# Warming matmuls up to the first scaled rows, and the first norm's factors on a queue of their own

## The chip, the cores and the metric

The kernel runs on one core of one Trainium2 chip. The metric is device time in microseconds (us) of one execution. TensorE (PE) multiplies, VectorE (DVE), ScalarE (ACT) and GpSimd (POOL) work on rows, SyncE (SP) issues DMAs. A core's engines have a queue each and meet through semaphores.

## The reference, cut

All arrays are float32: x is 1 x 512 x 1024, `w_in` 1024 x 6656, the feed-forward inner width 2816.

```python
h = rmsnorm(x, norm1_g)                       # y = x * rsqrt(mean(x^2) + eps) * g
z = h @ w_in + b_in
z_glu, z_rx, z_rg, z_ga, z_gb = split(z)
u = z_glu[:, :1024] * sigmoid(z_glu[:, 1024:])
u = silu(layernorm(causal_depthwise_conv(u, conv_dw_w, conv_dw_b)))
y_a = u @ conv_w_out + conv_b_out
hb = rg_lru(causal_depthwise_conv(z_rx, ...), ...)     # gates per head, a scan over time
y_b = (hb * gelu(z_rg)) @ lru_w_out
x = x + (sigmoid(z_ga) * y_a + sigmoid(z_gb) * y_b) @ w_mix_out
h = rmsnorm(x, norm2_g)
x = x + (silu(h @ ffn_w1) * (h @ ffn_w3)) @ ffn_w2
return rmsnorm(x, norm_f_g)
```

## The kernel before

Activations are kept with channels on partitions: a tile is 128 channels by 512 positions. Each factor of a product is split into a high part in TensorE's faster float32 form and a low part (the remainder), and a product is three matmuls per 128 channels (`mm3`): high by high, high by low, low by high. With `lo_last` the products with the weights' low part come last. Weights come in chunks of 128 x 1024 (`emit_chunk`): SP loads `raw_in`, ScalarE casts the high part (line 122), GpSimd or VectorE subtracts the low part (line 118).

The change lies in the head of the kernel, up to the end of the first four products.

- `load_x(t)`: SP loads rows 128t to 128t+127 of x in two halves of 512 columns.
- `norm1_rows(t)`: ScalarE sums squares over both halves (lines 530 and 536), then takes the square root (537); VectorE inverts it (538) and scales the rows in place (570).
- `turn_half("tx", ...)`: for half of the positions (two t's) and each of the eight channel tiles, TensorE turns two 128 x 128 blocks (554); ScalarE writes the high part h1kh times the norm's factor (557) and VectorE the low part h1kl (558). The factor is a column of `par`.
- `par`: all vectors of parameters, one column per 128 channels. They are loaded as rows (`load_rows`) into row tiles `rows`, turned by TensorE and copied out by VectorE (`rows_turned`, lines 498 and 499). The first row tile holds `norm1_g` (8 rows) and `b_in` (52 rows).
- `early_mm(i, hf)`: the first four products z, each on half of the positions.
- The warming matmuls (line 486) multiply a tile of ones by itself ahead of all that; nobody reads what they write.

In the head the order on PE, ACT, DVE and SP is the one written out by hand (`tc.manual_schedule`); further on a scheduler decides it. SP's queue before: x of t = 0 and 1, the rows of `norm1_g`, the rows of `b_in`, the first two weight chunks, x of t = 2 and 3, a third chunk, all other parameter rows, then more chunks. TensorE's: 12 warming matmuls, the turning of `norm1_g` and `b_in`, tx of the first half, z of two chunks, tx of the second half, z of two more, the turning of all other parameters, and the four products' second halves. In ScalarE's, the cast of the first weight chunk stands between the sums of squares and the factors of tx.

Of the kernel before, what the change touches and what calls it, by code (L numbers as in the profile page):

```python
# [13 lines left out]
P = 128  # L14
# [19 lines left out]
RAW = 4  # L34
HL = 5
AHEAD = 4
WARM = 12

FEW, MANY = 32, 112

# [12 lines left out]
ROWS = [  # L53
    ("norm1_g", 8), ("b_in", 52), ("conv_dw_b", 8), ("conv_ln_g", 8), ("conv_ln_b", 8),
    ("conv_b_out", 8), ("lru_conv_b", 10), ("lru_ba", 10), ("lru_bx", 10),
    ("lru_lambda", 10), ("norm2_g", 8), ("lru_conv_w", 40),
    ("conv_dw_w", 248),
]
# [27 lines left out]
def tile_block(ctx, tc, a, out):  # L86
    nc = tc.nc
# [18 lines left out]
    def bank(name):  # L106
        return psum.tile([P, T], F32, tag="mm", name=name)

    def bank2(name):
        return psum2.tile([P, T], F32, tag="cv", name=name)  # L110

    vec, act, pe, pool_e = nc.vector, nc.scalar, nc.tensor, nc.gpsimd
# [56 lines left out]
    def emit_to(n):  # L169
        while emitted[0] < min(len(chunks), n):  # L170
            emit_chunk()
# [271 lines left out]
    n_rows = sum(n for _, n in ROWS)  # L443
    n_first = ROWS[0][1] + ROWS[1][1]
    par = consts.tile([P, n_rows], F32, name="par")
    row_at = lambda c: (0, c) if c < n_first else (1 + (c - n_first) // P, (c - n_first) % P)
    at, col, parts = 0, {}, []
    for name, n in ROWS:
        col[name] = at
        src = a[name]  # L450
        src = src.rearrange("l k (c p) -> (l k c) p", p=P) if len(src.shape) == 3 else src.rearrange("l (c p) -> (l c) p", p=P)
        done = 0
        while done < n:
            m = min(n - done, P - row_at(at + done)[1])
# [2 lines left out]
        at += n  # L457
    rowt = [longt(f"rows{b}") for b in range(row_at(n_rows - 1)[0] + 1)]

    def load_rows(i):  # L460
        lo, m, src = parts[i]
        b, r = row_at(lo)
        nc.sync.dma_start(rowt[b][r : r + m, :P], src)

    x_nat = a["x"].rearrange("b (t p) d -> p (b t) d", p=P)
    xt = [[longt(f"x{t}{h}") for h in range(2)] for t in range(NT)]
# [1 line left out]
    def load_x(t):  # L468
        for h in range(2):
            nc.sync.dma_start(xt[t][h], x_nat[:, t, h * T : (h + 1) * T])  # L470

    eps_t = consts.tile([P, 1], F32, name="eps_t")
    vec.memset(eps_t, EPS)
# [10 lines left out]
    wp = bank2("warm")  # L484
    for _ in range(WARM):
        pe.matmul(wp[:, :P], ones, ones, start=True, stop=True)

    first = [i for i, (lo, _, _) in enumerate(parts) if lo < n_first]
    load_x(0)
    load_x(1)  # L490
    for i in first:
        load_rows(i)

    def rows_turned(c0, c1):
        pt = bank2(f"par_ps{c0}")
        for c in range(c0, c1, P):
            m = min(P, c1 - c)
            pe.transpose(pt[:, c - c0 : c - c0 + m], rowt[row_at(c)[0]][:m, :P], ident[:m, :m])
        vec.tensor_copy(par[:, c0:c1], pt[:, : c1 - c0])
# [5 lines left out]
    def mm3(ps, ws, xs, lo_last=False):  # L505


        n = 3 * len(ws)
        i = 0
        three = [((wh, xh), (wh, xl), (wl, xh)) for (wh, wl), (xh, xl) in zip(ws, xs)]  # L510
        if lo_last:
            three = [q[:2] for q in three] + [q[2:] for q in three]
        for l, r in (q for qs in three for q in qs):
            pe.matmul(ps, l, r, start=i == 0, stop=i == n - 1)  # L514
            i += 1

    def w_tiles(key, kt, ahead=AHEAD):
        h, l = weights(key, ahead)
        return [(h[:, k, :], l[:, k, :]) for k in range(kt)]
# [21 lines left out]
    def rstd_of(halves, junk, between=None):  # L541
        begun = rstd_begin(halves[0], junk[0])
        if between:
            between()
        return rstd_end(begun, halves[1], junk[1])

    def turn_half(name, rows, gname, dest, hf, bk, some=range(ND)):

        cs = slice(hf * 256, hf * 256 + 256)
        for c in some:  # L550
            ps = bk[c % len(bk)](f"{name}{hf}{c}")
            for t in range(2):
                src = rows[2 * hf + t][c // 4][:, (c % 4) * P : (c % 4 + 1) * P]
                pe.transpose(ps[:, t * P : (t + 1) * P], src, ident)
            g = pc(gname, c)
            h, l = (v[:, cs] for v in dest[c])
            act.activation(h, ps[:, :256], AF.Copy, scale=g)
            last = vec.scalar_tensor_tensor(out=l, in0=ps[:, :256], scalar=g, in1=h.bitcast(F32), op0=ALU.mult, op1=ALU.subtract)
        return last.ins

    def parts_of(pair_tiles, cs=slice(0, T)):
        return [(h[:, cs], l[:, cs]) for h, l in pair_tiles]
# [3 lines left out]
    def norm1_rows(t):  # L566
        junk = [shortt(f"n1j{t}{h}") for h in range(2)]
        r = rstd_of(xt[t], junk)
        for h in range(2):
            vec.tensor_scalar(out=xt[t][h], in0=xt[t][h], scalar1=r, scalar2=None, op0=ALU.mult)  # L570
# [6 lines left out]
    def early_mm(i, hf):  # L577
        m = EARLY_IN[i]
        if hf == 0:
            early.append((m, w_tiles(f"in{m}", ND, 0), bank(f"z{m}")))  # L580
        _, ws, ps = early[i]
        mm3(ps[:, HALVES[hf]], ws, parts_of(h1p, HALVES[hf]), lo_last=hf == 0)
# [3 lines left out]
    with tc.manual_schedule(engines={ET.PE, ET.Activation, ET.DVE, ET.SP}):  # L586
        norm1_rows(0)
        norm1_rows(1)
        rows_turned(0, n_first)
        emit_to(1)  # L590
        turn_half("tx", xt, "norm1_g", h1p, 0, [bank, bank, bank, bank2])
        emit_to(2)
        load_x(2)
        load_x(3)
        norm1_rows(2)
        norm1_rows(3)
        emit_to(3)
        for i in range(len(parts)):
            if i not in first:
                load_rows(i)  # L600
        early_mm(0, 0)
        early_mm(1, 0)
        turn_half("tx", xt, "norm1_g", h1p, 1, [bank2, bank, bank])
        emit_to(4)
        early_mm(2, 0)
        early_mm(3, 0)
        rows_turned(n_first, n_rows)
        for i in range(4):
            early_mm(i, 1)
# [447 lines left out]
    first = {}  # L1057
# [189 lines left out]
```

## Time and profile before

| | us |
|---|---|
| median of 3 runs | 807.54 |
| lowest, highest | 807.03, 810.36 |
| the profiled execution | 807.57 |
| its span, first to last instruction | 805.8 |

A row of a timeline gives the start and the length in us, the engine, the line and the operation, out<-in by the program's names, and in brackets how long the engine had sat idle and what ended that. A row of the chain gives start, length, engine, what and line. A row of stretches gives the stretch, its length, the busy time of engines with the count of their records in brackets, then TensorE's granted clock as a share of full speed, the mean busy share of the DMA engines, and GB/s. Where a line is given, PE and PEld (the loads of weights into TensorE) are of that line alone. PEq, SPq and the like are an engine's own sequencer.

### The profile page before, as it was taken

Reading aid. Unit: us, or ns where it says so; the run is one execution under the profiler, and the core shown is the slowest. Engines: PE = TensorE matmul, PEld = TensorE weight load, DVE = VectorE, ACT = ScalarE, POOL = GpSimd, SP = SyncE. Lnnn points to the kernel's source line nnn. Section 1 sums busy time; section 2 is a strip of 40 time slices with the busy share of each in tenths; the row PEclk is TensorE's granted clock in tenths of the full one; section 3 lists DMA queues with packets and bytes.
Section 4 is the critical chain, followed back from the end, with each engine's and each line's share of the span. In section 5 each row is a group of like instructions: output and inputs, shape, how many; then the busy total and the mean of one; then the engine's idle time right before and its main releaser. Section 6 shows DMA issues by size and latency. Waiting matters only on the chain.

```text
span 805.8 us, 12192 instructions
## 1 busy us (share of the span) xinstructions
PE 790.4 (98%) x4374; PEld 690.7 (86%) x4374; DVE 677.6 (84%) x1026; ACT 471.4 (58%) x677; POOL 234.3 (29%) x184
## 2 busy tenths in 40 slices
PE   8999999999999999999999999999999999999996
PEld 7988888788888888888888888999999999888885
DVE  4699899999989988786788879887878887889756
ACT  7546585988668855563326474454555555577443
POOL 3565867786766855130000000000000000000000
PEclk8999999999999999999999999999999999999999
DMA  7945547377564764468847546667555543676652
GB/s 216 231 122 164 172 149 213 118 233 206 168 188 151 221 179 119 127 207 266 279 155 236 157 130 164 153 160 202 153 141 132 132 131 105 209 260 198 197 169 105
DMA packets 184912, 141.34 MB, mean 175 GB/s; under 512 B 14311, under 2 KB 162195, under 8 KB 184851
## 3 DMA queue, kind: packets, MB, share of 16 engines
q1 hardware_dynamic: 183123, 134.27, 54.9%
q0 software_dynamic: 1728, 6.29, 4.1%
q8 instruction: 34, 0.56, 0.3%
q14 instruction: 27, 0.22, 0.1%
HBM read 113.79 MB, written 18.64 MB: 164 GB/s over the span
## 4 chain that ended last, share of the span: by engine, by line
PE 80%; DVE 8%; DMA 6%; ACT 3%; issue 2%; SPq 0%; ACTq 0%; DVEq 0%; POOLq 0%
PE z L514 29%; PE or L926 13%; PE yb L514 7%; PE fa L1052 6%; PE ft L1052 6%; PE ya L514 5%; PE mxr L926 5%; DMA raw_fb<-raw_fb 3%; DVE cv L673 3%; PE fe L1052 3%; PE fb L1052 2%; DMA raw_fb<-in_ffn_w_dram 2%; PE g L800 2%; PE fr L1052 1%; DVE raw_fb L346 1%
## 5 line engine op out<-in xcount | busy, mean ns | idle before, releaser
L673 DVE SCALAR_TENSOR_TENSOR cv<-u,par,cv 128x511 f32<-128x511 f32 (+16 forms) x240 | 162.1, 729 | 2.7 <-ACT cv L670 2.5
L118 POOL TENSOR_TENSOR hl_in<-raw_in,hl_in 128x1024 fp32r<-128x1024 f32 x52 | 126.0, 2428 | 81.4 <-ACT hl_in L122 78.4
L344 POOL DMA_DIRECT2D raw_fb<-raw_fb x12 | 10.5, 873 | 301.3 <-DMA raw_fb<-in_ffn_w_dram 134.6
L118 POOL TENSOR_TENSOR ows<-ows 128x256 f32<-128x256 f32 x66 | 57.4, 872 | 37.3 <-DMA ows<-in_ffn_w_dram 34.3
L122 ACT CAST hl_ft<-raw_fb 128x1024 fp32r<-128x1024 f32 x40 | 41.7, 1049 | 31.3 <-DVE raw_fb L346 16.7
L122 ACT CAST hl_in<-raw_in 128x1024 fp32r<-128x1024 f32 x52 | 54.2, 1043 | 9.5 <-PE z L514 6.6
L118 DVE TENSOR_TENSOR hl_ft<-raw_fb,hl_ft 128x1024 fp32r<-128x1024 f32 x40 | 48.5, 1218 | 9.3 <-ACT hl_ft L122 9.2
L118 DVE TENSOR_TENSOR hl_fb<-raw_fb,hl_fb 128x1024 fp32r<-128x1024 f32 x30 | 36.6, 1221 | 9.0 <-ACT hl_fb L122 8.8
L514 PE MATMUL z<-h10h,hl_in 128*128 128x512 f32 (+1 forms) x112 | 42.3, 379 | 0.0
L514 PE MATMUL z<-h11h,hl_in 128*128 128x512 f32 (+1 forms) x112 | 41.8, 375 | 0.0
L514 PE MATMUL z<-h14h,hl_in 128*128 128x512 f32 (+1 forms) x112 | 41.8, 375 | 0.0
L514 PE MATMUL z<-h13h,hl_in 128*128 128x512 f32 (+1 forms) x112 | 41.8, 375 | 0.0
L514 PE MATMUL z<-h12h,hl_in 128*128 128x512 f32 (+1 forms) x112 | 41.8, 375 | 0.0
L514 PE MATMUL z<-h15h,hl_in 128*128 128x512 f32 (+1 forms) x112 | 41.8, 375 | 0.0
L514 PE MATMUL z<-h16h,hl_in 128*128 128x512 f32 (+1 forms) x112 | 41.7, 374 | 0.0
L514 PE MATMUL z<-h17h,hl_in 128*128 128x512 f32 (+1 forms) x112 | 41.7, 374 | 0.0
L122 ACT CAST hl_fb<-raw_fb 128x1024 fp32r<-128x1024 f32 x30 | 31.4, 1046 | 10.9 <-PE f L514 5.8
L346 DVE TENSOR_TENSOR raw_fb<-raw_fb,raw_fb 128x1024 f32<-128x1024 f32 x18 | 22.0, 1225 | 18.4 <-DMA raw_fb<-in_ffn_w_dram 18.1
L122 ACT CAST hl_ob<-raw_ob 128x1024 fp32r<-128x1024 f32 (+1 forms) x23 | 23.4, 1015 | 20.2 <-PE or L926 9.8
L118 DVE TENSOR_TENSOR hl_ob<-raw_ob,hl_ob 128x1024 fp32r<-128x1024 f32 (+1 forms) x23 | 26.9, 1171 | 9.2 <-ACT hl_ob L122 9.2
L1052 PE MATMUL fe<-hs_0h,hl_ft 128*128 128x256 f32 x160 | 30.7, 284 | 0.2 <-ACT hs_0h L122 0.2
L1052 PE MATMUL ft<-hs_1h,hl_ft 128*128 128x256 f32 x160 | 30.4, 283 | 0.0
(960 smaller groups left out, 2616.8 us busy)
## 6 DMA issues: line engine op xcount, KB each, us to landing
raw_in<-in_w_in_dram SPq DMA_DIRECT2D x52, 512.0 KB
raw_fb<-in_ffn_w_dram SPq DMA_DIRECT2D x96, 256.0 KB
ows<-in_ffn_w_dram SPq DMA_DIRECT2D x44, 256.0 KB
os<-ows SPq DMA_DIRECT2D x22, 512.0 KB
raw_ob<-in_ffn_w_dram SPq DMA_DIRECT2D x33, 256.0 KB
raw_ot<-os SPq DMA_DIRECT2D x33, 256.0 KB
raw_fb<-raw_fb POOLq DMA_DIRECT2D x12, 512.0 KB, 4.5
raw_lo<-in_lru_w_out_dram SPq DMA_DIRECT2D x16, 320.0 KB
```

The source lines that it names most:

```text
L118: return eng.tensor_tensor(out=o, in0=x, in1=y, op=ALU.subtract)
L122: copy(h, full)
L344: pool_e.dma_start(out=q, in_=y, accum_op=ALU.add)
L346: vec.tensor_tensor(out=q, in0=q, in1=y, op=ALU.add)
L514: pe.matmul(ps, l, r, start=i == 0, stop=i == n - 1)
L673: vec.scalar_tensor_tensor(out=acc[c][:, s:], in0=u[c][:, : T - s], scalar=dw(c, s), in1=acc[c][:, s:], op0=ALU.mult, op1=ALU.add)
L800: pe.matmul(ps, l, r, start=k == 0, stop=k == len(mms) - 1)
L926: pe.matmul(banks[i], l_[:, ts], r_, start=start and n == 0, stop=stop and n == 2, skip_group_check=again)
L1052: pe.matmul(ps[:, HALVES[i]], lw[:, 4 * i + c, :], rx_, start=not (again or i or c or m), stop=bool(i and c == 3 and m == 2), skip_group_c ...
```

## The change

Twenty-one warming matmuls in place of twelve. `norm1_g` gets a row tile of its own, and its load is issued by ScalarE's queue, as the first thing there. `b_in`'s rows get a tile too; SP loads them behind x of t = 2 and 3, and TensorE turns them ahead of the other parameters, behind the first halves of the four early products. The first turning has 8 rows in place of 60.

```diff
-WARM = 12
+WARM = 21
...
-    row_at = lambda c: (0, c) if c < n_first else (1 + (c - n_first) // P, (c - n_first) % P)
+    starts = (0, ROWS[0][1], n_first)
+
+    def row_at(c):
+        b = sum(c >= s_ for s_ in starts) - 1
+        return b + (c - starts[b]) // P, (c - starts[b]) % P
...
-    def load_rows(i):
+    def load_rows(i, queue=nc.sync):
         lo, m, src = parts[i]
         b, r = row_at(lo)
-        nc.sync.dma_start(rowt[b][r : r + m, :P], src)
+        queue.dma_start(rowt[b][r : r + m, :P], src)
...
+    first = [i for i, (lo, _, _) in enumerate(parts) if lo < n_first]
+    load_rows(first[0], act)
...
-    first = [i for i, (lo, _, _) in enumerate(parts) if lo < n_first]
     load_x(0)
     load_x(1)
-    for i in first:
-        load_rows(i)
...
         norm1_rows(0)
         norm1_rows(1)
-        rows_turned(0, n_first)
+        rows_turned(0, ROWS[0][1])
         emit_to(1)
         turn_half("tx", xt, "norm1_g", h1p, 0, [bank, bank, bank, bank2])
         emit_to(2)
         load_x(2)
         load_x(3)
+        for i in first[1:]:
+            load_rows(i)
         norm1_rows(2)
         norm1_rows(3)
...
         early_mm(2, 0)
         early_mm(3, 0)
+        rows_turned(ROWS[0][1], n_first)
         rows_turned(n_first, n_rows)
```

## The prediction

> **What bounds the kernel now.** I read the page first, then the chain of waits of the first 60 us, the waits of TensorE (PE) up to 50 us, and then TensorE's clock stretch by stretch.
>
> ```profile
> span 805.8 us, 12192 instructions
> PE 790.4 (98%) x4374; PEld 690.7 (86%) x4374; DVE 677.6 (84%) x1026; ACT 471.4 (58%) x677; POOL 234.3 (29%) x184
> ```
>
> TensorE is busy for 98% of the span. So a microsecond taken from its path at the front is worth about a microsecond at the end, unless a later stage takes it back. All that the change touches lies in the first 28 us. Their chain (start, length, what):
>
> ```profile
> 6.55 0.61 ACT n1j L530 x2
> 7.16 0.66 ACT n1j L536 x2
> 8.37 0.50 DVE x L570
> 8.91 3.46 PE tx L554 x15
> 12.37 6.76 PE z L514 x48
> 19.13 2.13 PE tx L554 x16
> 27.24 0.32 PE par_ps L498 x3
> ```
>
> The path runs through the loads and the sums of squares on ScalarE to the scaled rows, and from 8.91 us on through TensorE alone: the first transposes (tx, first half of the columns of time), the first two products z, the second half's transposes, and on. What TensorE waited for before:
>
> ```profile
> PE par_ps L498 <- DMA rows<-in_b_in_dram: 2.1, 1, 2.1
> PE tx L554 <- DVE x L570: 0.6, 1, 0.6
> ```
>
> The 2.1 us lie ahead of 7.66 us, and nothing late came of that wait itself: the scaled rows come only at 8.9. Its price is in the clock. Five stretches (length, PE busy with its records, granted clock, DMA share, GB/s):
>
> ```profile
> 0.92:4.33 3.41, 3.24 (x15) 1.00 0.62 196
> 4.33:7.74 3.41, 1.31 (x12) 1.00 1.00 304
> 7.74:11.15 3.41, 2.85 (x13) 0.50 1.12 340
> 11.15:14.57 3.42, 3.42 (x18) 0.50 0.88 254
> 14.57:17.98 3.41, 3.41 (x30) 1.00 0.15 39
> ```
>
> I cut them at the places where the clock changes: it falls to 0.50 at 7.74, and returns at 14.57, twice 3.41 us later. The pace says what that is worth. Rows by line: the warming matmuls (L486, two records to a matmul), the products (L514), the transposes (L554), each once at either clock; the count in a row also holds what had begun before it and still ran: one record, two in the second and fourth, none in the sixth.
>
> ```profile
> 1.46:4.23 2.77, 2.77 (x14) 2.77 (x14) 1.00 0.75 237
> 4.39:5.28 0.89, 0.89 (x10) 0.89 (x9) 1.00 0.84 292
> 12.38:14.30 1.92, 1.92 (x10) 1.92 (x10) 0.50 0.85 213
> 15.13:18.85 3.72, 3.72 (x33) 3.72 (x32) 1.00 0.24 63
> 9.17:11.95 2.78, 2.78 (x14) 2.78 (x14) 0.50 1.05 368
> 18.97:20.17 1.20, 1.20 (x11) 1.20 (x12) 1.00 1.05 302
> ```
>
> The first row began 13 records: 2.77 / 13 = 0.213 us each. The second: 0.89 / 8 = 0.111. Products: 1.92 / 9 = 0.213 at half clock, 3.72 / 31 = 0.120 at full. Transposes: 2.78 / 13 = 0.214 and 1.20 / 11 = 0.109. So TensorE also stood at half clock before 4.33, though the row says 1.00, and went to full after a stretch that was 3.24 / 3.41 = 95% busy. A stretch that was 1.31 / 3.41 = 38% busy cost it the clock again, and one that was 84% busy, with transposes nearly all of it, did not bring it back.
>
> **The change part by part.**
>
> *Nine more warming matmuls*, 18 records.
>
> ```profile
> 1.09 4.47 PE L486 MATMUL warm<-ones 128*128 128x128 f32 x24 [1.09 <-DVE ones L479]
> 7.66 0.28 PE L498 MATMUL par_ps<-ident,rows 60*128 60x60 f32 x1 [2.10 <-DMA rows<-in_b_in_dram]
> L735 ACT ACTIVATE sg<-z,par x8: 679/689/692, 33.4 to 232.3; 128x512 f32<-128x512 f32 x8
> ```
>
> The 24 records of before end at 1.09 + 4.47 = 5.56. Eighteen more at 0.111 are 2.0 us: they end at 7.56. They stand in TensorE's queue ahead of the turning of the factors and of tx, neither of which can go on before 8.91, so they delay nothing; they fill the second stretch from 1.31 to about 3.2 us, 94%. I take it that the clock is then not cut at 7.74.
>
> *The factors of the first norm on ScalarE's queue, b_in behind the x loads.* These rows show the issues, ScalarE's work around them, and the steps up to the products:
>
> ```profile
> 2.14 0.28 ACT L481 CAST onesr<-ones 128x128 fp32r<-128x128 f32 x1
> 2.60 0.38 SPq L463 DMA_DIRECT2D rows<-in_norm_g_dram  x1
> 3.03 0.31 SPq L463 DMA_DIRECT2D rows<-in_b_in_dram  x1
> 3.38 1.03 SPq L156 DMA_DIRECT2D raw_in<-in_w_in_dram  x2
> 3.38 0.63 ACT L530 ACTIVATE n1j<-x 128x512 f32<-128x512 f32 x1 [0.96 <-DMA x<-in_x_dram]
> 8.88 1.05 ACT L122 CAST hl_in<-raw_in 128x1024 fp32r<-128x1024 f32 x1 [0.75 <-DMA raw_in<-in_w_in_dram]
> 9.16 0.21 DVE L499 COPY par<-par_ps 128x60 f32<-128x60 f32 x1
> 9.84 0.47 ACT L557 ACTIVATE h10h<-tx,par 128x256 fp32r<-128x256 f32 x1
> 10.34 0.48 DVE L558 SCALAR_TENSOR_TENSOR h10l<-tx,par,h10h 128x256 fp32r<-128x256 f32 x1 [0.96 <-ACT h10h L557]
> 13.09 0.48 DVE L558 SCALAR_TENSOR_TENSOR h17l<-tx,par,h17h 128x256 fp32r<-128x256 f32 x1
> 17.66 0.88 DVE L570 TENSOR_SCALAR x<-x,stats 128x512 f32<-128x512 f32 x2
> 27.08 0.48 PE L498 MATMUL par_ps<-ident,rows 128*128 128x128 f32 x3
> ```
>
> No DMA of ScalarE stands in this trace. By SP's rows an issue holds its engine 0.31 to 0.38 us; ScalarE's first work then moves back by that much and `onesr` ends at about 2.8 instead of 2.42. The 0.96 us that ScalarE waits for x covers it, so I cost it at nothing; were it 1.3 us, 0.3 us of it would show. The load has until 7.6 to land, and b_in's rows, which used to be turned with it, are first used as a bias at 33.4 (the L735 row).
>
> On SP the weights and the second half of x are issued 3.38 - 2.60 = 0.78 us earlier. The DMA share was 1.00 and 1.12 in the stretches where they land, so they may land earlier by anything from 0 to 0.78. ScalarE's cast of raw_in sat 0.75 us for that load, and h10h stands right behind the cast. With the load earlier, h10h waits next for the copy of the factors, which VectorE does after its scaling, at 9.16 + 0.21 = 9.37. I put h10h at 9.40: 0.44 us earlier, the work of ScalarE and VectorE behind it too. Lower bound 0.
>
> *What TensorE gains.* Sixteen transposes at 0.109 from 8.91 end about 10.55 instead of 12.37, and z follows when h10l is there, 10.82 - 0.44 = 10.38; so z starts at about 10.66 instead of 12.02. It then goes on in pairs, one for each h1k, for which VectorE takes (13.09 - 10.34) / 7 = 0.39 us each.
>
> Now the clock again. The stretch from 7.74 to 11.15 will hold transposes, a wait, and at most 0.5 us of products. In the row of before, 84% of transposes did not raise the clock. I take it that such a stretch does not keep it up either, and that the cut comes at 11.15. [...]
>
> With the cut: two pairs by 11.15, six pairs at 2 x 0.213 to 13.71, then the eight low-part products, four at half clock to 14.57 and four at 0.12 to 15.05, then the second product's 24 at 0.12, 2.88 us, to 17.93. The transposes of the second half start there instead of at 18.97. Their rows must be scaled by then: the row at 17.66 holds two scalings of 0.44, tx wants the first, so 18.10 before and 17.66 with the 0.44 gained on ScalarE and VectorE. That is just met. The start moves from 18.97 to 17.95 with the hand-over: 1.02 us. *Back goes* b_in's turning, which is now one more transpose and copy at 27 us on TensorE's path: three took 0.32 in the chain, one is 0.11. The copy (0.21) lies on VectorE, ahead of work that waited until then anyway. All else is issued in the same order as before.
>
> The sum: 1.02 - 0.11 = 0.91 us. The profiled execution took 807.57 us beside its span of 805.8, and the median of the runs is 807.54, so nothing has to be shifted: 807.57 - 0.91 = 806.7.
>
> **The rivals.**
>
> *Never cut:* transposes do keep the clock. Then the two products no longer bind, and tx waits for the scaled rows, 17.66 against 18.97: 1.31 less 0.11, or 1.2 us: 806.4. If the loads land the whole 0.78 earlier and the sums of squares follow, up to another 0.4: 806.0. Without the earlier load, the rows are there at 18.10, the gain is 0.87 - 0.11, and it is 806.8.
>
> *Taken back later:* TensorE waits again in a stage where other engines set the pace.
>
> ```profile
> 87.25 16.34 PE z L514 x72
> 104.20 0.61 ACT hl_gate L122
> 160.93 1.40 PE g L800 x5
> ```
>
> From 104 to 161 us the chain is ScalarE's and VectorE's, until g at 160.93. If that stage does not end earlier, the gain is gone and it is 807.6, with b_in's transpose hidden too. Against it: the chain enters that stage from TensorE (87.25 + 16.34), not from a load that keeps its own time.
>
> *Overrun (slower):* the 21 matmuls end too late. They do so when the clock is raised late. Raised at 4.33 they end at 7.56; raised one stretch later, at 7.74, 31 records are done at 0.213 and 11 follow at 0.111, to 8.97, which is about when the scaled rows come: that is the point from which it costs. Not raised at all, 42 x 0.213 = 8.96 us, to 10.05, then the factors' turning (0.28 in the L498 row above) before tx at 10.33 instead of 8.91; h10h follows two transposes and a 0.2 us hand-over later, at about 10.95 instead of 9.84: 1.1 us, with 0.11 for b_in 1.2 lost: 808.8. Against it: 3.41 us of 95% raised it in this execution. [...]
>
> *Nothing done:* the clock is cut at 7.74 all the same and the loads land no earlier. Then only 0.11 is added, 807.7; it goes with "taken back".
>
> **How the numbers follow.** Forecast (cut at 11.15, 806.7; its own range 806.4 to 806.9): 0.42. Never cut (806.0 to 806.8): 0.25. Taken back or nothing done (807.2 to 808.0, the 0.5 us between the two lower runs around it): 0.20. Overrun (to 808.8): 0.11. Left 0.02 for what I don't see. A range from 805.8 to 808.0 holds the first three, 0.87, less what their own bounds miss: 0.8. A measurement of this kernel can tell some 0.5% from no change, 4 us. No case reaches that downwards: faster 0.01; upwards a long stall of a kind that I don't name: slower 0.02; same 0.97.
>
> **What would show it.** In the profile after: warming records up to about 7.6 us, and no wait for b_in; the granted clock still 1.00 at 8 us (if it is 0.50, the second step is wrong); transposes 0.11 us apart from 8.9 on; 0.50 from 11.15 to 14.57 and back (1.00 throughout: "never cut"); ScalarE's cast at 8.1 to 8.9 and h10h near 9.4; tx of the second half near 17.9; three plus one turnings at about 26. If tx starts there but the g at 160.93 does not come earlier by the same, it was taken back. Warming records at 0.21 us beyond 8.9 would be the overrun.

## The result, and the profile after

| | before | after |
|---|---|---|
| median of 22 runs each, us | 807.5 | 809.18 |
| lowest, highest | 806.7, 810.36 | 808.39, 811.4 |
| the profiled execution | 807.57 | 809.11 |
| its span | 805.8 | 807.3 |

The ratio after to before is 1.0022, with a 95% interval of [1.0015, 1.0029]. The change costs about 1.7 us by the medians. The forecast was 806.7, with a range up to 808.0: a small loss where a small gain was forecast. The medians and the two profiled executions differ alike (1.68 and 1.54 us), so the two traces can be set beside each other. Their difference comes in two places: the head gains little, and a place 480 us further on, which the diff does not touch, loses more.

**The head.** The timeline of the changed kernel (start, length, what):

```profile
1.09 7.20 PE L494 MATMUL warm<-ones 128*128 128x128 f32 x42 [1.09 <-DVE ones L487]
2.76 0.28 ACT L489 CAST onesr<-ones 128x128 fp32r<-128x128 f32 x1
3.61 0.63 ACT L535 ACTIVATE n1j<-x 128x512 f32<-128x512 f32 x1 [0.57 <-DMA x<-in_x_dram]
9.25 1.05 ACT L122 CAST hl_in<-raw_in 128x1024 fp32r<-128x1024 f32 x1 [0.76 <-DMA raw_in<-in_w_in_dram]
9.27 1.85 PE L559 MATMUL tx<-ident,x 128*128 128x128 f32 x15 [0.57 <-DVE x L575]
10.20 0.47 ACT L562 ACTIVATE h10h<-tx,par 128x256 fp32r<-128x256 f32 x1
11.24 0.39 PE L519 MATMUL z<-h10h,hl_in 128*128 128x256 f32 x1
```

The first 60 us of its chain end with the second half's transposes, products and the four turnings:

```profile
18.00 0.50 DVE x L575
18.54 2.24 PE tx L559 x15
20.78 5.96 PE z L519 x48
26.74 0.66 PE par_ps L503 x4
```

The stretches of TensorE's clock (stretch, length, PE, PEld, DVE, ACT, POOL busy, clock, DMA share, GB/s):

```profile
1.09:5.82 4.73, 4.73 (x22) 4.73 (x23) 0.15 (x1) 3.38 (x8) 0.22 (x1) 1.00 0.69 215
5.82:9.23 3.41, 2.88 (x24) 2.55 (x23) 1.87 (x7) 1.76 (x6) 0.00 (x0) 1.00 1.10 305
9.23:12.64 3.41, 3.25 (x23) 2.83 (x24) 2.38 (x7) 3.39 (x8) 2.26 (x1) 1.00 1.08 361
```

The wait of 2.1 us for b_in's rows is gone. The first row says 1.00, but its 22 records in 4.73 us, 0.215 us each, are the pace of half clock, as in before; from 5.82 us on the granted clock stays at 1.00 (to 804.5 us, behind the last matmul), and the transposes run 0.12 us apart (1.85 / 15) instead of 0.23. Yet the first scaled rows come 0.36 us later than before (tx at 9.27, not 8.91), the first z gains 0.78 us (11.24 for 12.02), the second half's tx 0.43 (18.54 for 18.97), and the turnings end at 27.40 instead of 27.56. That leaves 0.16 us, and those 0.16 stay: in the chain of after the g that began at 160.93 begins at

```profile
160.79 1.41 PE g L808 x5
```

**The loss.** Among TensorE's waits of after, one of 1.5 us has no counterpart in before, where th (the turning of the second norm's rows) waits once, 0.4 us, at 475.0 and for VectorE's rows. The waits at fr (a product of the feed-forward) are much the same, 1.4 us in after and 1.5 in before. The wait of 1.5 us:

```profile
PE th L559 <- DVE h24l L563: 1.5, 1, 1.5
```

The chain of after from 474 us on shows what lies behind it:

```profile
474.48 4.94 DMA raw_fb<-in_ffn_w_dram
...
480.88 1.23 DVE hl_fb L118
482.10 0.40 DVE h24l L563
...
482.55 0.45 PE th L559 x2
```

Between the load and hl_fb's low part stands the cast, in ScalarE's timeline of after:

```profile
479.80 1.05 ACT L122 CAST hl_fb<-raw_fb 128x1024 fp32r<-128x1024 f32 x1 [1.83 <-DMA raw_fb<-in_ffn_w_dram]
```

In ScalarE's timeline of before that cast starts without an idle time:

```profile
478.23 1.05 ACT L122 CAST hl_fb<-raw_fb 128x1024 fp32r<-128x1024 f32 x1
```

The load of a weight chunk of the feed-forward (raw_fb) ends late; its cast, its low part and h24l follow in order on ScalarE and VectorE, and th of TensorE waits 1.5 us for h24l. The load was issued 0.3 us earlier than before, and ends 1.3 us later (479.42 for 478.15 in the traces). At fr, the row of before at 549.29, after is 1.28 us behind, and near 743 us it loses another 0.3, whose cause stays open.

What else was on the DMA engines then? The queues in 476 to 478 us, first of after, then of before; then of before in 479.9 to 481.2 (packets, MB, share of 16 engines):

```profile
q1 hardware_dynamic: 774, 0.38, 64.4%
q8 instruction: 1, 0.02, 3.4%
```
```profile
q1 hardware_dynamic: 943, 0.47, 78.1%
...
q8 instruction: 1, 0.02, 4.5%
```

In after one packet of q8, the queue that the profile lists as `instruction`, falls into this load; in before the like falls at 480, behind it. It takes 0.034 x 16 x 2.0 = 1.1 us of one DMA engine. That this packet is what holds the load up shows in what remains when it is through, at 477.7 us. First two stretches of after, then one of before (busy times of PE, PEld, DVE, ACT, POOL, then clock, DMA share, GB/s):

```profile
478.00:478.50 0.50, 0.50 (x4) 0.36 (x3) 0.48 (x2) 0.00 (x0) 0.00 (x0) 1.00 0.07 11
478.50:479.00 0.50, 0.50 (x5) 0.47 (x4) 0.00 (x0) 0.00 (x0) 0.00 (x0) 1.00 0.06 15
...
478.00:478.50 0.50, 0.50 (x4) 0.13 (x3) 0.50 (x2) 0.50 (x2) 0.00 (x0) 1.00 0.00 0
```

A share of 0.06 to 0.07 is one engine of sixteen. The load reports its end in sixteen parts: in after fifteen are in by 477.88 and the last comes at 479.42, in before all come between 477.54 and 478.15. The two slow kernels below, e2 and e3, show the same: fifteen parts by 477.24 and 478.04, the last at 478.76 and 479.84.

The packet is the queue's 18th, and its place goes by TensorE's work: in all twelve kernels of this document 4511 to 4554 records of TensorE's queue stand ahead of it, though it comes at 468.3 us in one and at 480.6 in another. The page of after begins

```profile
span 807.3 us, 12230 instructions
```

which is 38 instructions more than the 12192 of before, 36 of them the warming matmuls' in TensorE's queue. So the packet comes earlier in the kernel's work, at 476.6 us instead of 480.0. I take q8's packets for fetches of TensorE's instructions, by the count: 34 packets, 0.56 MB in all, for the 8748 records of PE and PEld in before, 257 each. Below, a fetch is one of them, and "the fetch" is the 18th. At least one of the 34 packets of after has a cost that shows: the wait of 1.5 us.

### The profile page after: what moved, and what is told of

The parts are those of the page before. It is cut to its first block, busy times and chain, and to the rows that moved or that the text cites. A ratio compares the mean times of both kernels' runs of the same rounds, so it can differ in the third digit from the quotient of the medians.

```text
span 807.3 us, 12230 instructions
## 1 busy us (share of the span) xinstructions
PE 792.0 (98%) x4393; PEld 691.2 (86%) x4393; DVE 677.8 (84%) x1027; ACT 471.8 (58%) x677; POOL 233.7 (29%) x184
## 4 chain that ended last, share of the span: by engine, by line
PE 73%; DVE 12%; DMA 8%; ACT 3%; issue 2%; POOL 1%; SPq 1%; DVEq 0%; ACTq 0%; POOLq 0%
PE z L519 28%; PE or L934 8%; PE yb L519 7%; PE fa L1060 6%; PE ft L1060 6%; PE ya L519 5%; PE mxr L934 5%; DMA raw_fb<-raw_fb 3%; PE fe L1060 2%; DMA raw_fb<-in_ffn_w_dram 2%; DVE cv L681 2%; PE fb L1060 2%; PE g L808 2%; DVE hl_ob L118 1%; PE fr L1060 1%
```

## The experiments

*Theory of the fetch:* more TensorE instructions anywhere ahead move the fetch onto a load that TensorE will wait for. *Rivals:* the moved loads and the new queue; or the earlier arrival of the head at that stage. Each group of experiments has its own runs of before: median 807.51 for e1 to e4, 807.29 for f2 to f5, 807.55 for g1 and g2. Ratios are of that group's runs.

**e1: the whole change with the old count of matmuls.**

```diff
+    wide = gatet("wide")
+    vec.memset(wide, 1.0)
...
-    for _ in range(WARM):
-        pe.matmul(wp[:, :P], ones, ones, start=True, stop=True)
+    for i in range(12):
+        n = P if i < 6 else T
+        pe.matmul(wp[:, :n], ones, ones if i < 6 else wide, start=True, stop=True)
```

> The changed kernel, but its warming time (21 matmuls of 128 columns) is made of 12 matmuls, six of 128 and six of 512 columns, so TensorE's program has 36 instructions fewer ahead of everything else and all else is as in the changed kernel. Theory (fetch): a block of TensorE's own instructions is fetched over the same DMA engines after every so many instructions; the added ones moved one fetch onto the load of raw_fb at 474 to 478 us, whose last part then landed 1.5 us late. With the old count the fetch falls behind that load again, at about 480 us, and what the head gained stays: 0.3 to 0.5 us faster than before, about 807.1. Rival (queue and rows): the late landing comes from the loads that were moved or from the new queue, and stays: 1.5 to 1.9 us slower than before, about 809.2. Rival (shift): everything after the head comes 0.15 to 0.4 us earlier and this alone puts loads on each other: the same 809.2.

Median 808.25 (807.47 to 808.99), ratio 1.0005 [0.9996, 1.0013]; profiled execution 807.47. The wait of th is gone and the fetch stands at 479.9 us. The queue for the factors and the late b_in are all in it, so they do not bring the wait by themselves. The time missed the expected 807.1: the four turnings (L506 here) end level with before, so there was no gain of the head to keep, and the profiled execution is the fastest of the eleven runs, so that what puts the median 0.8 us above it stays open.

**e2: the loads of before, 21 short matmuls in the time of 12.**

```diff
-    for _ in range(WARM):
-        pe.matmul(wp[:, :P], ones, ones, start=True, stop=True)
+    for i in range(21):
+        n = P if i < 8 else 39
+        pe.matmul(wp[:n, :n], ones[:, :n], ones[:, :n], start=True, stop=True)
```

> The kernel before, but its warming time (12 matmuls of 128 columns) is made of 21 matmuls, eight of 128 and thirteen of 39 columns by 39 weights; nothing else differs, no load is moved. Theory (fetch): the instruction count alone moves the fetch by 36 instructions onto the load at 474 us: 1.3 to 2 us slower than before, about 809.3, with the wait of the cast of raw_fb at 478 to 480 us. Rivals (queue and rows, shift): neither queue nor loads nor the head's time has changed: as before, 807.5 within 0.3.

Median 808.71 (807.8 to 811.11), ratio 1.0012 [1.0002, 1.0021]. The fetch stands at 476.5 us, and first the chain, then TensorE's waits show the late load and the wait:

```profile
473.84 4.92 DMA raw_fb<-in_ffn_w_dram
```
```profile
PE th L555 <- DVE h24l L559: 1.1, 1, 1.1
```

Only the number and the size of the warming matmuls differ from before, and the wait comes, although the head gained about 0.9 us here. The median is 1.2 us above before, a little less than the 1.3 to 2 expected.

**e3: nothing but WARM = 21.**

```diff
-WARM = 12
+WARM = 21
```

> The kernel before with 21 warming matmuls of 128 columns and nothing else of the change. Theory (fetch): as the changed kernel or a little slower, 809 to 809.6. Rival (queue and rows): no slower than before, the clock kept in the head: 806.7 to 807.5. Rival (shift): slower only if the head is earlier: 807.5 to 809.2.

Median 808.73 (807.51 to 811.2), ratio 1.001 [0.9999, 1.002], an interval that just holds 1, and below the 809 to 809.6 expected; the profiled execution, 809.28, has the same two lines, of the chain and of the waits:

```profile
474.77 5.07 DMA raw_fb<-in_ffn_w_dram
```
```profile
PE th L554 <- DVE h24l L558: 1.3, 1, 1.3
```

**e4: the change without the added matmuls.**

```diff
-WARM = 21
+WARM = 12
```

> The changed kernel with 12 warming matmuls as before: the moved loads and the split rows alone. Theory (fetch): the count is that of before but for two instructions, so there is no late landing at 474 us; with the clock cut in the head as before it is within 0.5 us of before, 807 to 808. Rival (queue and rows): 1.5 to 1.9 us slower than before, about 809.2. Rival (shift): 807 to 808 as well.

Median 807.62 (806.62 to 810.25), ratio 0.9997 [0.9988, 1.0007]; fetch at 480.4, no wait at th. The queue and the rows by themselves change nothing that can be measured. With 12 matmuls the clock is lost in the head all the same:

```profile
2.75:6.16 3.41, 3.41 (x18) 3.41 (x17) 0.82 (x4) 2.49 (x8) 0.00 (x0) 1.00 0.88 257
6.16:9.57 3.41, 0.69 (x4) 0.36 (x3) 1.13 (x5) 1.30 (x6) 0.00 (x0) 1.00 1.13 312
9.57:12.98 3.41, 3.39 (x16) 3.39 (x17) 2.42 (x8) 3.41 (x8) 2.31 (x1) 0.50 1.05 352
```

**f2 and f3: the changed kernel with still more instructions**, to push the fetch past the load. The edits: 31 matmuls of 75 columns; 41 of 53.

```diff
-    for _ in range(WARM):
-        pe.matmul(wp[:, :P], ones, ones, start=True, stop=True)
+    for _ in range(31):
+        pe.matmul(wp[:75, :75], ones[:, :75], ones[:, :75], start=True, stop=True)
```

> The changed kernel with 31 warming matmuls of 75 columns in place of 21 of 128: about the same warming time, 40 more TensorE instructions. Theory (a block of TensorE's own instructions is fetched over the DMA engines, and its place goes by the count of instructions before it): 40 more at about 0.079 us each move the fetch from 476.6 us to about 473.5, between the load of raw_f (467.5 to 471.7) and that of raw_fb (475 to 478). The wait of th at 482 us (1.5 us) goes, and the median is 1.2 to 1.5 below the changed kernel's 809.2: 807.5 to 808.2. Rival (any instruction more than the kernel before has costs, or the changed head arrives at that stage at a bad time): the wait stays, 809.2 or more.

> The changed kernel with 41 warming matmuls of 53 columns in place of 21 of 128: about the same warming time, 80 more TensorE instructions. Theory of the fetch: it moves to about 470.5 us, onto the load of raw_f that ends at 471.7. The wait at 482 us goes, and one of up to 1.5 us comes at the cast of hl_f at 472 and behind it on TensorE; 808.5 to 809.3. If there is slack behind that earlier load, less: down to 807.5. Rival (each added instruction costs): the wait of 482 us stays, above 809.2.

f2: 810.25 (809.41 to 812.4), ratio 1.0036 [1.0022, 1.005]. f3: 810.65 (809.27 to 811.45), 1.0034 [1.002, 1.0047]. Both times missed what the theory gave, while its local claim held: the fetches stand at 472.4 and 468.3 us, the wait at 482 is gone, and f2's load of raw_fb takes its 3.5 us again. But the later fetches moved too, and time is lost further on. First f2's chain and TensorE's waits, then before's chain at the same load and at fr:

```profile
474.91 3.50 DMA raw_fb<-in_ffn_w_dram
...
515.57 4.16 DMA raw_fb<-in_ffn_w_dram
...
550.78 4.63 PE fr L1060 x24
```
```profile
PE fr L1060 <- ACT ft L1142: 2.4, 1, 2.4
```
```profile
510.11 4.53 DMA raw_fb<-raw_fb
...
515.18 3.51 DMA raw_fb<-in_ffn_w_dram
...
549.29 3.13 PE fr L1052 x24
```

f2's load at 515.57 takes 4.16 us for 3.51 of before, and a fetch stands just ahead of it, at 514.9. That the fetch lengthens it is not shown: it is through at 515.9, the load's first data move at 516.2, and its parts do not end with one alone far behind, as in after. TensorE reaches fr 1.5 us late, after a wait of 2.4 us where before waits 1.5. That wait then costs the clock, and fr another 4.63 - 3.13 = 1.5 us. The stretches of f2:

```profile
548.13:551.54 3.41, 1.03 (x9) 0.83 (x8) 2.55 (x3) 1.53 (x2) 0.00 (x0) 1.00 1.09 287
551.54:554.95 3.41, 3.41 (x18) 3.41 (x18) 2.88 (x3) 1.59 (x3) 0.86 (x1) 0.50 0.30 77
```

In f3 fetches stand at 511.1 and 733.0 us. Its chain, its queue of instructions in 510.4 to 516.1 and in 732.8 to 738.3, and TensorE's wait:

```profile
510.45 5.62 DMA raw_fb<-raw_fb
...
733.24 5.00 DMA raw_ot<-os
```
```profile
q8 instruction: 1, 0.02, 1.0%
...
q8 instruction: 1, 0.02, 1.1%
```
```profile
PE or L934 <- DVE x2b L887: 1.0, 1, 1.0
```

The adding transfer takes 5.62 us for 4.53 of before, and it has the mark of after: fifteen of its parts end by 514.97 us, the last at 516.07. TensorE then waits 2.3 us at fr, for 1.5 in before. The load of raw_ot takes 5.00 us for 3.92 in f2 and in f4 (below), which have no fetch there; but the packet is through at 733.9, when the load's data have just begun (733.8), and the parts end spread out, so the fetch as its cause is not shown. Nor does every hit cost so much: with the fetch at 468.3 in f3 the load of raw_f takes 4.34 us, beside 3.98 to 4.24 in the other kernels, and TensorE does not wait for it. So the loss of f2 and f3 as a whole is explained in part only, and their medians leave open that many added instructions cost in other ways too.

**f4: the loads of before, 12 matmuls, 6 of them 512 wide**, and **f5: the change with 9, 8 of them wide**, to warm long with few instructions. In f5 the edit is e1's, with 9 and 1 in place of 12 and 6:

```diff
+    for i in range(12):
+        n = P if i < 6 else T
+        pe.matmul(wp[:, :n], ones, ones if i < 6 else wide, start=True, stop=True)
```

> The kernel before with its 12 warming matmuls, 6 of them 512 columns wide: warming to about the same time as the changed kernel, the instruction count and all loads as before. Theory of the fetch: it stays at about 480 us, no wait at 482; the head gains about 0.3 us as with 21 matmuls alone: 806.9 to 807.4. Rival (the earlier end of the head is what brings the wait): 808.5 or more.

> The changed kernel with 9 warming matmuls, 8 of them 512 columns wide: 48 TensorE instructions fewer than it has, 12 fewer than the kernel before. Theory of the fetch: it moves to about 481 us, after the load of raw_fb; no wait at 482; 807.3 to 808.2, as with 12 of the same warming time. Rival (moved loads bring the wait): 809.2.

f4: 807.77 (807.07 to 808.94), ratio 0.9999 [0.999, 1.0009]; f5: 808.55 (807.7 to 809.84), 1.0013 [1.0005, 1.0021]. Neither has the wait at 482, as the theory says. Both were dearer than expected, and in both the warming overran: in f4 it ends at 10.2 us. In f5 the clock rose at 5.78 us, and the timeline shows that the warming matmuls end at 10.8 us, behind the scaled rows:

```profile
1.67 9.13 PE L497 MATMUL warm<-wide,ones 128*128 128x512 f32 x16
```

The chain of f5 runs through them, and it is about 1.0 us behind before from 28 us on. f4 is level with before there (0.1 us behind). In f4's chain stands the load named above:

```profile
731.45 3.92 DMA raw_ot<-os
```

**g1 and g2: the dose.** The loads of before, with 9 matmuls, 3 of them 512 wide (the loop above with `range(9)` and 6); and WARM = 15.

> The kernel before with 9 warming matmuls, 3 of them 512 columns wide, in place of 12 of 128: more warming time, 12 TensorE instructions fewer, all loads as before. Theory of the fetch: the block goes from 480.0 us to about 481, clear of the load of raw_fb (478.2): no wait at 482; the warming ends before 9 us even if the clock is raised late, so the head gains 0 to 0.9 us: 806.6 to 807.5. Rival (an earlier head is taken back in the stage at 474 to 483 whatever the count): 808 or more.

> The kernel before with 15 warming matmuls of 128 columns: 12 TensorE instructions more, a third of the way to the changed kernel's 36. Theory of the fetch: the block goes from 480.0 us to about 479.0, still behind the load of raw_fb (478.2): no wait at 482, and the load takes 3.5 us as with the old count: 806.8 to 807.6. Rival (each added matmul costs its share): a third of the loss, a wait of about 0.5 us, 807.9.

g1: 807.02 (805.91 to 809.07), ratio 0.9992 [0.9983, 1.0002], the lowest of all, though its interval holds 1. Its profiled execution, 806.55, has a head 0.8 us earlier than before and keeps that: the cast of hl_fb comes without idle time (TensorE's and ScalarE's timelines).

```profile
3.81 3.31 PE L489 MATMUL warm<-wide,ones 128*128 128x512 f32 x6
8.79 1.86 PE L557 MATMUL tx<-ident,x 128*128 128x128 f32 x15 [0.68 <-DVE x L573]
```
```profile
477.41 1.05 ACT L122 CAST hl_fb<-raw_fb 128x1024 fp32r<-128x1024 f32 x1
```

g2: 807.53 (806.77 to 809.35), 1.0001 [0.9993, 1.001]. Its fetch stood at 477.4 us, not at the 479.0 expected, but the load, too, was earlier and had just ended (477.44), so the cast of hl_fb started at 477.52 without a wait: no third of the loss, so for the wait at 482 us the place counts and not so much per matmul. Its head, too, is 0.8 us earlier, and a wait of TensorE near 741 us takes that back (its waits). No fetch of TensorE's stands there (713.4 and 746.3 are the nearest), and the chain from 729 us to that wait is VectorE's work, with no transfer in it: a gain can be lost further on without the fetch.

```profile
PE or L926 <- DVE x2b L879: 0.6, 1, 0.6
```

| kernel | TensorE instructions against before | fetch near 480, us | inside the load of raw_fb? | wait of th at 482, us |
|---|---|---|---|---|
| before, e1, e4, f4 | 0 to +2 | 479.7 to 480.4 | no | none |
| g1, f5 | -12, about -10 | 479.1, 480.6 | no | none |
| g2 | +12 | 477.4 | no, at its end | none |
| after, e2, e3 | +36 to +38 | 476.5 to 477.5 | yes | 1.5, 1.1, 1.3 |
| f2, f3 | about +80, +120 | 472.4, 468.3 | no | none |

The theory of the fetch stands for the wait at 482 us; both rivals fall for it, the loads by e2 and e3, which have the wait without them, and by e4, the earlier head by g1 and g2. It explains the loss in the traces of after, e2 and e3; what f2 and f3 lose further on it explains in part only, and the losses near 741 to 743 us in g2 and after it does not.

## Why the prediction was wrong

- **Nine more matmuls "delay nothing".** This is the step that failed. It held for what stands behind them in TensorE's queue, up to their end at 8.29, and left out that they are instructions themselves: the 34 packets of q8 are on the DMA engines that also carry the weights, and with 36 more records the 18th came at 476.6 us, in the load of raw_fb, instead of at 480.0. Cost: from 0.16 us ahead to 1.54 behind, about 1.7 us, nearly all of it the wait of th. The other part of the miss is the head, which gained 0.16 us where 0.91 was forecast; the next points say why.
- **End of the warming, 7.56 us.** They ended at 1.09 + 7.20 = 8.29, since the clock rose at 5.82 and not at 4.33. The conclusion, no cut in the next stretch, was right, but with other edges than the forecast's: the stretch from 5.82 to 9.23 was 2.88 / 3.41 = 84% busy. The rise came at 3.94, 5.78, 6.16, 7.05 and 7.11 us in e1, f5, e4, e3 and e2, so the 4.33 of one profiled execution could not be carried over to the others.
- **ScalarE's issue at nothing.** `onesr` ended at 3.04, not at the 2.8 forecast; ScalarE still waited 0.57 us for x, so the cover held.
- **Loads 0.44 us earlier.** They did not come: the first sum of squares began 0.23 us later (3.61 for 3.38), the cast of the first weight chunk 0.37 later (9.25 for 8.88), h10h at 10.20 instead of the forecast 9.40. My lower bound, 0, excluded a loss without a reason. None of the six kernels with the moved loads has h10h ahead of before's 9.84 (9.95 to 10.49, and 11.37 in f5). Why x itself lands later is not settled, and the moved loads need not be the reason: the first sum of squares begins at 3.41 to 3.88 with them and at 3.38 to 3.84 without.
- **The cut at 11.15.** Wrong: the rival "never cut" happened. In the stretch of after from 9.23 to 12.64 transposes are 1.85 of the 3.25 busy us, and the clock stayed. e2 says it more sharply, where PE was busy for 2.20 of 3.41 us (64%), all of it with transposes:

```profile
7.11:10.52 3.41, 2.20 (x17) 1.76 (x16) 1.51 (x5) 1.98 (x5) 0.66 (x1) 1.00 1.09 336
```

  So in these two stretches transposes counted towards keeping the clock: without them e2's stretch would be idle, and one of 38% lost the clock in before, one of 20% (0.69 of 3.41) in e4. Raising it went otherwise, in one stretch of each kind: in e1 a stretch that was 84% busy with warming matmuls (2.85 of 3.41 us up to the rise at 3.94, its start counted back) raised the clock, and the prediction's stretch of transposes, busy for the same 2.85 us, did not. The prediction took the one for the other.
- **The second half 1.02 us earlier.** It came 0.43 earlier, and something else set it: not the products, as forecast, but the scaled rows, as in the rival "never cut". They are there at 18.50; the forecast had them at 17.66, from the earlier loads that did not come, and the rival's 18.10 without earlier loads was too early as well. A slip in the sum had no effect: sixteen transposes at 0.109 from 8.91 end at 10.65, not 10.55, and the 10.66 at which z was put follows from that.
- **b_in's turning 0.11 us.** It took 0.34: four turnings 0.66, three had taken 0.32.
- **Rivals.** "Taken back later" named the wrong stage: at g, 161 us, the 0.14 us of that time were kept. "Overrun" did not decide in after, but it is what f5 shows, about 1 us, with longer matmuls than the rival had in mind. "Within 0.5%" was right; the sign inside it was not, and 809.2 lies above the range. The runs also tell smaller changes from none than the 0.5% assumed: 0.22% is clear of 1 here.

## What to carry to other kernels

The added instructions cost more here than their time on their engine: 36 to 38 more on TensorE moved its 18th fetch from 480.0 us to 476.5 to 477.5. Where TensorE was busy for 98% of the span and a load came just in time, a fetch on that load cost waits of 1.1 to 1.5 us, 470 us behind the added instructions. So look in the trace at where the instruction queue's packets fall against the loads that the chain runs through, before and after. Warming with few long instructions in place of many short ones left the fetch at 479.1 to 480.6 us here, behind the load (e1, f4, f5 and g1); g1 did so without overrunning and had the lowest median, though not clear of noise. And with a small gain in the head, compare the chain stage by stage to the end before believing that it is kept.

## What the hardware did that I had not expected

- One packet of 0.02 MB on one of 16 DMA engines (1.1 us) made a load of 3.5 us take 4.9 to 5.1 us: fifteen engines were done and the sixteenth was 1.5 to 1.8 us behind. In f3 the like lengthened another transfer by 1.1 us.
- A wait 0.9 us longer took the clock with it: 2.4 us of wait in f2 left a stretch 30% busy (1.03 of 3.41), and the next 3.41 us ran at 0.50. In f3 a wait of 2.3 us at the same place did not: counted on from its rise at 6.83 in steps of 3.4133 us (f2's changes at 5.40 and 551.53 are 160 of them apart, 546.13 / 160; those of before at 14.57 and 803.05 are 231, 788.48 / 231), a stretch ends inside the wait, at 549.55, and the two stretches are 79% and 54% busy by this estimate.
- In these traces the clock was kept by a stretch 64% busy, at full clock, and lost by those 20, 30 and 38% busy; at half clock one 84% busy with the prediction's transposes did not raise it, one 84% busy with warming matmuls did (e1, by its start counted back), and so did those of 95% and more.
